# Streaming encoder step in two-pass memory attention form: splits, evictions, a row buffer, writes and norms moved to other engines and places

## The chip, the cores and the metric

One NeuronCore of a Trainium2 chip runs the whole program. The metric is the device time of one execution in microseconds (us). The core has five engines that run in parallel, each through a list of its own in fixed order: TensorE (PE, with a separate weight-load row PEld), VectorE (DVE), ScalarE (ACT), GpSimd (POOL) and SyncE (SP), which only issues transfers. 16 DMA engines move data between SBUF and HBM.

## What is computed

One layer of a streaming encoder for 2048 prompt frames and 8 x 16 sample frames of width 1024, all in float32. Cut to its core:

```
x = x + rmsnorm(y_mix, g_mix_post)           # y_mix: band attention + conv module, one output projection
h = rmsnorm(x, g_mem_pre)
x = x + rmsnorm(memory_attention(h, mk, mv, w_mq, w_mo), g_mem_post)
h = rmsnorm(x, g_ffn_pre)
f = (silu(h @ w_gate) * (h @ w_up)) @ w_down
x = x + rmsnorm(f, g_ffn_post)

def memory_attention(h, mk, mv, w_mq, w_mo):     # 4 heads of 256, 256 memory tokens
    q = h @ w_mq                                 # by heads
    s = einsum("bthd,bmhd->bhtm", q, mk) * 256 ** -0.5
    p = softmax(s)
    return (einsum("bhtm,bmhd->bthd", p, mv)) @ w_mo
```

mk and mv are rmsnorm(mem) @ w_mk and @ w_mv of the memory tokens. They and the updated caches are outputs too.

## The kernel before

**Numbers in two parts.** Every float32 operand of a matmul is split into hi (rounded to the format fp32r, by ScalarE) and lo (the rest, by VectorE or POOL, hi subtracted from the value). `mm3` issues three matmuls for each pair of operands: hi by hi, hi by lo, lo by hi (L268, L269, L270). A "form" below is such a pair of tiles.

**Seven products.** Large products are 2 x 2 blocks done with seven block products instead of eight. Each needs sums and differences of quarters of both operands; those of the weight side are b-forms, w-forms in the FFN, and those of the rows are a-forms, t-forms in the FFN.

**Who orders what.** The code is written engine by engine with tiles and pools; a scheduler then fixes the order of each engine's list. Tiles that share a place in SBUF (a `Region` gives each tag its places, in KiB, used in turn) wait for each other. An engine and SyncE's queue never overtake in their own lists: what waits holds up all behind it.

**Stages.** They follow one another, with the next one's first loads and forms let in early.

- `phase_mem` (0 to about 110 us). w_mk times the memory rows. Then w_mq is folded into mk, per head h of 4: `wload` (L256) loads two rows of w_mqT, ScalarE casts hi (L261), `lo_engine` subtracts lo (L263); 8 PSUM tiles of 6 matmuls each are evicted into `fo` times the gain (L436, VectorE). `keep(h, fo, of)` writes quarters to the HBM buffer `fs[0]`, and for heads 2 and 3 forms four sums of quarters (L401, POOL), each written too. Then w_mv and the fold of w_mo into mv, to `fs[1]`.
- `phase_proj`, attention (about 110 to 860).
- `mixout` with `cross_sample` woven in (about 860 to 1137): per tile i of 128 rows the output projection, the post-norm into the row tile `po` (L1058, VectorE), the residual added (L1059, POOL), and the write of x1 to HBM by POOL's queue (L1060). `po` has one place.
- `phase_cross` (about 1115 to 1500): 16 steps s of two row tiles each, some 22 us a step. Steps 0 to 7 multiply normed rows with the folded mk (scores), take the softmax and write it to `zs`; steps 8 to 15 multiply it with the folded mv and finish rows. `raw` loads half a b-form (L1215), `bform(halves_, j, engine)` makes form j in two halves: cast by ScalarE (L1223), lo by the engine passed (L1224). The seven b-forms of pass one are made ahead of step 0, out of loads `f1`, five ahead; those of pass two during step 7 in `between(j)`, out of loads `f2`. `aforms` makes the seven a-forms of the next step (casts L1265; lo L1266, on VectorE or POOL). `softmax` and `rows_out` are generators, stepped after every product. In `softmax` VectorE takes the maximum (L1307), ScalarE the exponentials with their sums (L1310), VectorE the reciprocals (L1313) and four scalings by head (L1315), and SyncE writes the rows (L1316). `rows_out` forms y, adds the residual (L1332) and writes the row of x2 (L1333, SyncE); in the last two steps (`done is None`) it ends there, else the normed row goes on to `forms_out`, which writes its FFN quarters to `hn`.
- For the rows that `forms_out` doesn't take, `natural(g, p)` reads x2 back (L1372), norms it (L1375 to L1379) and forms and writes quarters (POOL: L1380, L1382, L1384, L1386 with the issues between). (2, 2) is called in one piece in step 3; (2, 0) and (2, 1) are left in `self.todo`.
- `gate_up` (about 1490 to 2440): row groups g of 3, each over 22 blocks f of the hidden width. `tform` loads pieces of `hn` into the tag `nat` (L1519, three places), transposes and splits them (L1522, L1524, L1525). `wforms(f)` loads w_gate and w_up (L1531, L1532), POOL forms four sums (L1539 to L1542), ScalarE and VectorE split (L1544, L1545). In g = 0 an entry of `self.todo` is made whole behind f = 1 and f = 3. The turn to the next g re-makes the t-forms.
- `down` (about 2440 to the end).

Some of these lines shift in the changed file: L1333 there is L1332, L1519 is L1522, L1531 and L1532 are L1534 and L1535.

Of the kernel before, what the change touches and what calls it, by code (L numbers as in the profile page):

```python
# [17 lines left out]
P = 128  # L18
# [6 lines left out]
MH = 4  # L25
NM = 256
# [110 lines left out]
class Build:  # L137
# [214 lines left out]
    def phase_mem(self):  # L352
        nc, A = self.nc, self.A
# [15 lines left out]
        gk = self.t(pool, [P, KC], F32, "gk")  # L369
# [18 lines left out]
        def keep(h, fo, of):  # L388

            c, sub = h % 2, nc.gpsimd.tensor_tensor  # L390
            part = lambda j: self.fs[0][:, j, :, c * 256:(c + 1) * 256]
            temp = lambda tag: self.t(pool, [P, 4, 256], F32, tag)[:, :, :]
            if h < 2:
                nc.sync.dma_start(part(0), fo[:, :4, :])
                nc.sync.dma_start(part(2), fo[:, 4:, :])
                return
            (b11, b21), (b12, b22) = [(x[:, :4, :], x[:, 4:, :]) for x in (of[c], fo)]
            nc.sync.dma_start(part(6), b22)
            t1, t3, t2, t4 = temp("t1"), temp("t3"), temp("t1"), temp("t3")
            for j, t, x, y in ((4, t1, b12, b11), (3, t3, b22, b12), (1, t2, b22, t1), (5, t4, t2, b21)):  # L400
                sub(t, x, y, ALU.subtract)  # L401
                nc.sync.dma_start(part(j), t)

        for which, wn, on in ((0, "w_mk", "new_mem_k_promptT"), (1, "w_mv", "new_mem_v_promptT")):
            yh = self.t(pool, [P, KC, NM], F32R, "yh", 2)
            yl = self.t(pool, [P, KC, NM], F32R, "yl", 2)
            scale = 1.0 / 16.0 if which == 0 else 1.0
            for j in range(KC):
# [5 lines left out]
                ps = self.t(ps_mm, [P, 512], F32, "mm")  # L414
# [9 lines left out]
            if which == 0:  # L424
                of = []
                for h in range(MH):
                    ws = [self.wload(A["w_mqT"][2 * h + c]) for c in range(2)]
                    fo = self.t(pool, [P, KC, NM], F32, "fo")
                    of.append(fo)
                    for ic in range(KC):  # L430
                        ps = self.t(ps_mm, [P, 512], F32, "mm")
                        cc = slice(ic * P, (ic + 1) * P)
                        for c in range(2):
                            self.mm3(ps[:, :NM], ws[c][0][:, cc], ws[c][1][:, cc],
                                     yh[:, 2 * h + c, :], yl[:, 2 * h + c, :], c == 0, c == 1)
                        nc.vector.tensor_scalar(fo[:, ic, :], ps[:, :NM], gk[:, ic:ic + 1], None, ALU.mult)  # L436
                    keep(h, fo, of)
# [542 lines left out]
    def mixout(self, ctx):  # L980
# [4 lines left out]
                .at("ct", 2, (ff, [2, 10])).lay(ff, 0, ("an", 2, 1)).lay(ff, 5, ("po", 4, 1)).at("spo", 4, (ff, [22]))  # L985
# [204 lines left out]
    def phase_cross(self, ctx):  # L1190
# [27 lines left out]
        def bform(halves_, j, engine):  # L1218
            hi = self.t(pool, [P, 4, 512], F32R, f"b{j}h")
            lo = self.t(pool, [P, 4, 512], F32R, f"b{j}l")  # L1220
            for x in range(2):
                wf, c = next(halves_), slice(2 * x, 2 * x + 2)
                nc.scalar.copy(hi[:, c, :], wf[:, :, :])  # L1223
                engine.tensor_tensor(lo[:, c, :], wf[:, :, :], hi[:, c, :].bitcast(F32), ALU.subtract)  # L1224
            return hi, lo
# [74 lines left out]
        def softmax(z, t, parts):  # L1300
# [13 lines left out]
            for h in range(MH):  # L1314
                nc.vector.tensor_scalar(z[:, h, :], z[:, h, :], ri[:, h:h + 1], None, ALU.mult)  # L1315
            nc.sync.dma_start(self.zs[t], z[:, :, :].rearrange("p h n -> p (h n)"))  # L1316

        def rows_out(y, x, t, parts, done):
# [14 lines left out]
            nc.sync.dma_start(self.x2[t], x[:, :])  # L1333
# [30 lines left out]
        def natural(g, p):  # L1364
# [5 lines left out]
            for x, (t, r0) in zip((xa, xb), PAIRS[g][p][:2]):  # L1370
# [7 lines left out]
                nc.gpsimd.tensor_tensor(r[:n, :], r[:n, :], self.mhalf[:n, 0:1], ALU.pow)  # L1378
                nc.vector.scalar_tensor_tensor(x2, x2, r[:n, :], gffn[:n, :], ALU.mult, ALU.mult)  # L1379
            nc.gpsimd.tensor_tensor(tt[:, 0, :], xb[:, 0, :], xa[:, 0, :], ALU.subtract)  # L1380
            nc.gpsimd.dma_start(dst[:n, p, 0:2, :], xa)
            nc.gpsimd.tensor_tensor(tt[:, 1, :], xb[:, 1, :], tt[:, 0, :], ALU.subtract)  # L1382
            nc.gpsimd.dma_start(dst[:n, p, 4:6, :], tt)
            nc.gpsimd.tensor_tensor(xb[:, 0, :], xb[:, 1, :], xb[:, 0, :], ALU.subtract)  # L1384
            nc.gpsimd.dma_start(dst[:n, p, 2:4, :], xb)
            nc.gpsimd.tensor_tensor(xa[:, 1, :], tt[:, 1, :], xa[:, 1, :], ALU.subtract)  # L1386
            nc.gpsimd.dma_start(dst[:n, p, 6, :], xa[:, 1, :])

        self.natural = natural
# [3 lines left out]
        bf = [bform(f1, 0, nc.vector)]  # L1393
# [4 lines left out]
        bf.append(bform(f1, 1, nc.vector))  # L1398
        src[1] = fetch(1)
        for j in range(2, 7):  # L1400
            next(gen, None)
            bf.append(bform(f1, j, nc.gpsimd if j % 2 == 0 else nc.vector))
# [4 lines left out]
        for s in range(2 * n):  # L1407
# [15 lines left out]
            def between(j):  # L1423
                if j >= 0 and s == n - 1:
                    nbf.append(bform(f2, j, nc.gpsimd if j % 2 else nc.vector))
# [3 lines left out]
                if j == 4 and s == 3:  # L1429
                    self.natural(2, 2)  # L1430
# [54 lines left out]
        self.todo = [(2, 0), (2, 1)]  # L1485
# [9 lines left out]
    def gate_up(self, ctx):  # L1495
# [5 lines left out]
        pool = (Region().at("wf", 4, (sbF, [24, 28, 34.5, 38.5])).at("s", 2, (sbF, [14, 20, 22])).at("nat", 2, (sbF, [8, 10, 12]))  # L1501
# [57 lines left out]
        for g in range(3):  # L1559
            n = sum(p[2] for p in PAIRS[g])  # L1560
            for fp in range(NF // 2):
# [4 lines left out]
                for x in range(2):  # L1566
# [47 lines left out]
                    if g == 0 and x == 1 and self.todo:  # L1614
                        self.natural(*self.todo.pop(0))
# [240 lines left out]
```

## Time and profile before

| | |
|---|---|
| runs of before (median, lowest, highest of 3) | 2919.37, 2910.35, 2920.2 us |
| profiled execution, its own time | 2914.59 us |
| its span, from the first to the last instruction | 2912.8 us |
| mean granted TensorE clock | 0.993 |
| busy share of PE, DVE, ACT, POOL | 97%, 75%, 47%, 52% |
| DMA moved | 533 MB, mean 183 GB/s |

The profile is one execution, recorded by the hardware profiler. A row of instructions names the engine, the line of the kernel, out<-in, the tile's shape and a count; a bracket at the end is the idle time of the engine just before it and what released it. Memories are named by their region: sbf, sbr and sbx are parts of SBUF, flexb the parts that stages share out anew, psb is PSUM. "issue" in the chain is time in which the engine waited for nothing that the profile shows.

### The profile page before, as it was taken

The numbers are of one execution on the slowest core, as the hardware profiler recorded it, in microseconds if no ns is written. First come the engines' busy times: TensorE is split into PE (matmuls) and PEld (weight loads), VectorE is DVE, ScalarE is ACT, GpSimd is POOL, SyncE is SP. The second block draws the span as 40 slices with busy tenths as digits, with TensorE's granted clock in tenths as the row PEclk, the third lists the DMA queues.
The fourth block names the chain that finished last, engine by engine and source line by source line (L and its number), as shares of the span: only waits on it lengthen the run. The fifth ranks groups of instructions, "written<-read, shape, count | busy, mean of one in ns | idle before, by whom it ended". The sixth has DMA issues, their size and how long they took to land.

```text
span 2912.8 us, 44818 instructions
## 1 busy us (share of the span) xinstructions
PE 2835.8 (97%) x16056; PEld 2559.9 (88%) x16056; DVE 2172.3 (75%) x3232; ACT 1383.4 (47%) x2779; POOL 1506.3 (52%) x1339
## 2 busy tenths in 40 slices
PE   9999999999999998999989999999999999999998
PEld 8899999988887676788779999999999999888786
DVE  7796785889884355778778778788889997555656
ACT  4535364678883245665443333433344444332433
POOL 3458396741123447537656656455556774324413
PEclk9999999999999999999999999999999999999999
DMA  8826253576635766546664333644344446657664
GB/s 280 295 76 201 94 170 119 187 239 217 226 100 183 264 220 207 176 167 242 224 229 169 131 115 126 201 151 157 124 165 137 144 144 226 226 174 224 221 218 148
DMA packets 214818, 533.02 MB, mean 183 GB/s; under 512 B 20633, under 2 KB 95257, under 8 KB 206266
## 3 DMA queue, kind: packets, MB, share of 16 engines
q1 hardware_dynamic: 206082, 482.57, 49.9%
q0 software_dynamic: 8512, 47.58, 4.5%
q8 instruction: 126, 2.06, 0.3%
q14 instruction: 98, 0.80, 0.1%
HBM read 383.28 MB, written 154.89 MB: 185 GB/s over the span
## 4 chain that ended last, share of the span: by engine, by line
PE 75%; DVE 7%; DMA 7%; issue 4%; POOL 4%; ACT 2%; SPq 0%; DVEq 0%; POOLq 0%; ACTq 0%
PE psb L270 21%; PE psb L268 21%; PE psb L269 21%; PE psb L276 5%; PE psb L869 2%; PE psb L838 2%; PE psb L856 1%; DMA sbf<-in_w_down_dram 1%; POOL sbf L1667 1%; DMA sbf<-x 1%; DVE psb L526 1%; DVE sbr L1545 1%; DMA sbf<-hn 1%; PE psb L1522 1%; PE psb L1118 1%
## 5 line engine op out<-in xcount | busy, mean ns | idle before, releaser
L268 PE MATMUL psb<-sbr 128*128 128x384 f32 (+3 forms) x2812 | 959.3, 344 | 12.8 <-DVE flexb L436 3.8
L269 PE MATMUL psb<-sbr 128*128 128x384 f32 (+3 forms) x2644 | 898.7, 340 | 0.2
L270 PE MATMUL psb<-sbr 128*128 128x512 f32 (+2 forms) x1852 | 655.6, 355 | 3.1 <-DVE sbr L1737 2.9
L268 PEld LDWEIGHTS psb<-sbr 128*128 128x128 f32 x2812 | 530.0, 189 | 50.9 <-ACT sbr L1736 5.2
L269 PEld LDWEIGHTS psb<-sbr 128*128 128x128 f32 x2644 | 499.5, 189 | 27.0 <-DVE sbr L318 0.4
L270 PE MATMUL psb<-sbr,sbx 128*128 128x384 f32 (+3 forms) x1400 | 459.0, 329 | 2.6 <-POOL sbx L263 1.6
L1544 ACT CAST sbr<-sbf 128x512 fp32r<-128x512 f32 x360 | 222.3, 620 | 397.2 <-PE psb L269 332.5
L1545 DVE TENSOR_TENSOR sbr<-sbf,sbr 128x512 fp32r<-128x512 f32 x360 | 354.9, 988 | 52.5 <-ACT sbr L1544 51.7
L270 PEld LDWEIGHTS psb<-sbr 128*128 128x128 f32 x1852 | 347.8, 188 | 39.3 <-DVE sbr L1737 7.1
L270 PEld LDWEIGHTS psb<-sbr,sbx 128*128 128x128 f32 x1400 | 266.0, 190 | 9.9 <-POOL sbx L263 1.8
L526 DVE SCALAR_TENSOR_TENSOR psb<-sbf,psb 128x768 f32<-128x768 f32 (+1 forms) x290 | 264.2, 911 | 6.2
L1737 DVE TENSOR_TENSOR sbr<-sbf,sbr 128x384 fp32r<-128x384 f32 (+2 forms) x242 | 166.6, 712 | 84.4 <-ACT sbr L1736 83.4
L263 POOL TENSOR_TENSOR sbx<-sbf,sbr 128x1024 fp32r<-128x1024 f32 (+1 forms) x62 | 151.6, 2447 | 98.6 <-ACT sbr L261 87.4
L1667 POOL TENSOR_TENSOR sbf<-sbf 128x512 f32<-128x512 f32 x77 | 104.7, 1366 | 167.9 <-DMA sbf<-in_w_down_dram 159.4
L1736 ACT CAST sbr<-sbf 128x384 fp32r<-128x384 f32 (+2 forms) x242 | 111.6, 482 | 156.7 <-PE psb L269 129.0
L536 POOL TENSOR_TENSOR flexb<-flexb,flexb 128x128 f32<-128x128 f32 (+1 forms) x180 | 171.2, 951 | 20.6 <-ACT flexb L535 11.1
L268 PE MATMUL psb<-sbr,sbx 128*128 128x384 f32 (+2 forms) x440 | 155.6, 354 | 8.8 <-ACT sbx L1265 6.6
L261 ACT CAST sbr<-sbf 128x1024 fp32r<-128x1024 f32 x98 | 102.1, 1049 | 119.9 <-PE psb L269 83.6
L1539 POOL TENSOR_TENSOR sbf<-sbf 128x512 f32<-128x512 f32 x66 | 94.4, 1430 | 113.8 <-DVE sbr L1545 71.6
L269 PE MATMUL psb<-sbr,sbx 128*128 128x384 f32 (+2 forms) x416 | 145.3, 349 | 0.0
L535 ACT ACTIVATE flexb<-sbf 128x128 f32<-128x128 f32 (+1 forms) x180 | 104.0, 585 | 69.7 <-POOL flexb L536 64.1
L269 PE MATMUL psb<-sbx,sbr 128*128 128x512 f32 (+2 forms) x376 | 134.6, 359 | 2.3 <-DVE sbx L1525 2.0
(353 smaller groups left out, 6191.3 us busy)
## 6 DMA issues: line engine op xcount, KB each, us to landing
af<-flexb SPq DMA_DIRECT2D x33, 1344.0 KB, 5.5
sbf<-in_w_down_dram SPq DMA_DIRECT2D x154, 256.0 KB, 3.8
sbf<-in_w_up_dram SPq DMA_DIRECT2D x66, 512.0 KB, 3.7
sbf<-in_w_gate_dram SPq DMA_DIRECT2D x66, 512.0 KB, 3.8
sbf<-af SPq DMA_DIRECT2D x85, 384.0 KB, 4.3
sbf<-x SPq DMA_DIRECT2D x53, 512.0 KB, 4.2
sbf<-in_w_in_dram SPq DMA_DIRECT2D x48, 512.0 KB, 4.5
sbr<-ks POOLq DMA_DIRECT2D x16, 1024.0 KB, 8.7
```

What stands on the lines that cost most here:

```text
L263: self.lo_engine.tensor_tensor(lo[:, c], wf[:, c], hi[:, c].bitcast(F32), ALU.subtract)
L268: nc.tensor.matmul(ps, lh, rh, start=start, stop=False, **kw)
L269: nc.tensor.matmul(ps, lh, rl, start=False, stop=False, **kw)
L270: nc.tensor.matmul(ps, ll, rh, start=False, stop=stop, **kw)
L276: nc.tensor.matmul(y[o], l, r[:, o * 512:(o + 1) * 512], start=start and x == 0, stop=stop and x == 2)
L526: nc.vector.scalar_tensor_tensor(acc if w < CW - 1 else o, src(w), cwt[:, j, w:w + 1], acc, ALU.mult, ALU.add)
L536: nc.gpsimd.tensor_tensor(o, o, v, ALU.add)
L1544: nc.scalar.copy(hs[j][:, :], src[j])
L1545: nc.vector.tensor_tensor(ls[j][:, :], src[j], hs[j][:, :].bitcast(F32), ALU.subtract)
L1667: nc.gpsimd.tensor_tensor(acc[:, :], acc[:, :], q[:, :], ALU.add if s > 0 else ALU.subtract)
L1736: nc.scalar.copy(ch[:, m], a[:, x, m])
L1737: nc.vector.tensor_tensor(cl[:, m], a[:, x, m], ch[:, m].bitcast(F32), ALU.subtract)
```

## The change

1. `keep`: the four sums of heads 2 and 3 (L401) move from POOL to VectorE. The fold's evictions (L436) move from VectorE's `tensor_scalar` to ScalarE's `activation` with a scale.
2. `mixout`: `po` gets a second place. Odd tiles i go to place 0 of sbF, i = 13 to 24, i = 15 to 28; these are also places of f1.
3. `bform`: all lo splits (L1224) go to VectorE. Before, forms 2, 4 and 6 of pass one and 1, 3 and 5 of pass two went to POOL.
4. `softmax`: the four scalings by head become one `tensor_tensor` of 128 x 1024 with the reciprocals broadcast along each head.
5. `rows_out`: in the last two steps the write of x2 is issued by POOL's queue. `nat` has seven places instead of three.
6. `natural` becomes a generator with a yield after each piece. (2, 2) is put among the tails in step 2 and stepped after each product; (2, 0) and (2, 1) are chained and stepped once per f of g = 0 from f = 3 on, at most 14 steps; the turn runs what is left.

```
-            c, sub = h % 2, nc.gpsimd.tensor_tensor
+            c, sub = h % 2, nc.vector.tensor_tensor
...
-                        nc.vector.tensor_scalar(fo[:, ic, :], ps[:, :NM], gk[:, ic:ic + 1], None, ALU.mult)
+                        nc.scalar.activation(fo[:, ic, :], ps[:, :NM], AF.Copy, scale=gk[:, ic:ic + 1])
...
-                .at("ct", 2, (ff, [2, 10])).lay(ff, 0, ("an", 2, 1)).lay(ff, 5, ("po", 4, 1)).at("spo", 4, (ff, [22]))
+                .at("ct", 2, (ff, [2, 10])).lay(ff, 0, ("an", 2, 1)).at("po", 4, *[(ff, [5]), (sbF, [0])] * 6, (ff, [5]), (sbF, [24]), (ff, [5]), (sbF, [28]), (ff, [5])).at("spo", 4, (ff, [22]))
...
-        def bform(halves_, j, engine):
+        def bform(halves_, j):
...
-                engine.tensor_tensor(lo[:, c, :], wf[:, :, :], hi[:, c, :].bitcast(F32), ALU.subtract)
+                tt(lo[:, c, :], wf[:, :, :], hi[:, c, :].bitcast(F32), ALU.subtract)
...
-            for h in range(MH):
-                nc.vector.tensor_scalar(z[:, h, :], z[:, h, :], ri[:, h:h + 1], None, ALU.mult)
+            tt(z[:, :, :], z[:, :, :], ri[:, :].unsqueeze(2).to_broadcast([P, MH, NM]), ALU.mult)
...
-            nc.sync.dma_start(self.x2[t], x[:, :])
+            (nc.sync if done is not None else nc.gpsimd).dma_start(self.x2[t], x[:, :])
...
+                yield
                 nc.vector.scalar_tensor_tensor(x2, x2, r[:n, :], gffn[:n, :], ALU.mult, ALU.mult)
+                yield
             nc.gpsimd.tensor_tensor(tt[:, 0, :], xb[:, 0, :], xa[:, 0, :], ALU.subtract)
             nc.gpsimd.dma_start(dst[:n, p, 0:2, :], xa)
+            yield
...
-                if j == 4 and s == 3:
-                    self.natural(2, 2)
+                if j == 1 and s == 2:
+                    tails.append(natural(2, 2))
...
-        self.todo = [(2, 0), (2, 1)]
+        self.todo = chain(natural(2, 0), natural(2, 1))
...
-.at("nat", 2, (sbF, [8, 10, 12]))
+.at("nat", 2, (sbF, [8, 10, 12, 46.5, 48.5, 42.5, 44.5]))
...
-                    if g == 0 and x == 1 and self.todo:
-                        self.natural(*self.todo.pop(0))
+                    if g == 0 and f > 2:
+                        next(self.todo, None)
+                    if turn:
+                        for _ in self.todo:
+                            pass
```

VectorE's list in the fold of heads 0 to 2, before (L263 are the lo splits of weight rows, L421 a split of the folded operand, L436 the evictions):

```order
L263 TENSOR_TENSOR sbx<-sbf,sbr 128x1024
L436 TENSOR_SCALAR flexb_173<-psb,flexb_169 128x256
L421 SCALAR_TENSOR_TENSOR sbr<-sbf,sbr 128x256
L436 TENSOR_SCALAR flexb_173<-psb,flexb_169 128x256 x7
L263 TENSOR_TENSOR sbx<-sbf,sbr 128x1024
L436 TENSOR_SCALAR flexb_173<-psb,flexb_169 128x256
```

and ScalarE's list at the same place, after:

```order
L420 ACTIVATE sbr<-sbf 128x256
L436 ACTIVATE flexb_173<-psb,flexb_169 128x256 x7
L261 CAST sbr<-sbf 128x1024
L261 CAST sbr<-sbf 128x1024
L436 ACTIVATE flexb_173<-psb,flexb_169 128x256 x8
L261 CAST sbr<-sbf 128x1024
```

The evictions now stand between ScalarE's casts of the weight rows; VectorE's list has the L263 and the four L401 of each of heads 2 and 3 there.

VectorE's list where mixout ends and cross begins, before (L1058 is the post-norm into po, L1224 the lo splits of b-forms, L1266 those of a-forms, L1272, L1277 and L1282 sums for a-forms):

```order
L1272 TENSOR_TENSOR flexb_9882<-psb,flexb_9882 128x512
L1058 SCALAR_TENSOR_TENSOR flexb_169<-psb,flexb_169,sbf 128x512 x2
L1224 TENSOR_TENSOR sbr<-sbf,sbr 128x1024 x4
L1266 TENSOR_TENSOR sbx<-psb,sbx 128x512
L1277 TENSOR_TENSOR flexb_9882<-flexb_9882,psb 128x512
L1282 TENSOR_TENSOR flexb_9882<-psb,flexb_9882 128x512
L1266 TENSOR_TENSOR sbx<-psb,sbx 128x512
L1224 TENSOR_TENSOR sbx<-sbf,sbr 128x1024
```

and after:

```order
L1272 TENSOR_TENSOR flexb_9882<-psb,flexb_9882 128x512
L1058 SCALAR_TENSOR_TENSOR sbf<-psb,flexb_169,sbf 128x512 x2
L1224 TENSOR_TENSOR sbr<-sbf,sbr 128x1024 x7
L1266 TENSOR_TENSOR sbx<-psb,sbx 128x512
L1277 TENSOR_TENSOR flexb_9882<-flexb_9882,psb 128x512
L1282 TENSOR_TENSOR flexb_9882<-psb,flexb_9882 128x512
L1058 SCALAR_TENSOR_TENSOR flexb_169<-psb,flexb_169,sbf 128x512 x2
L1224 TENSOR_TENSOR sbx<-sbf,sbr 128x1024
```

The post-norm of this tile writes to sbf instead of the one place in flexb_169, and seven splits instead of four stand between it and the first L1266.

SyncE's queue where cross ends and gate_up begins, before (x_12 to x_15 are the last rows of x2, L1519 the loads of hn pieces for the first t-forms):

```order
L1333 DMA x_14_84_156<-sbf 128x1024
L1532 DMA sbf<-in_w_up_dram 128x1024
L1333 DMA x_12_82_154<-sbf 128x1024
L1531 DMA sbf<-in_w_gate_dram 128x1024
L1519 DMA sbf<-hn_87_159 128x512 x3
L1531 DMA sbf<-in_w_gate_dram 128x1024
L1519 DMA sbf<-hn_87_159 128x512 x2
L1532 DMA sbf<-in_w_up_dram 128x1024
L1519 DMA sbf<-hn_87_159 128x512
L1333 DMA x_15_85_157<-sbf 128x1024
```

and after (L1522, L1534 and L1535 are the same loads):

```order
L1535 DMA sbf<-in_w_up_dram 128x1024
L1522 DMA sbf<-hn_87_159 128x512 x4
L1534 DMA sbf<-in_w_gate_dram 128x1024
L1522 DMA sbf<-hn_87_159 128x512 x5
L1534 DMA sbf<-in_w_gate_dram 128x1024
L1522 DMA sbf<-hn_87_159 128x512 x2
L1535 DMA sbf<-in_w_up_dram 128x1024
```

The four writes of x2 are gone from this queue (they stand in POOL's list), and the loads of hn and of the weights follow each other.

More of the change, by code (lines that the diff above doesn't have):

```diff
@@ L1 @@
 from contextlib import ExitStack
-from itertools import islice
+from itertools import chain, islice
 import concourse.bass as bass
@@ L1397, in phase_cross @@
         next(gen)
-        bf.append(bform(f1, 1, nc.vector))
+        bf.append(bform(f1, 1))
         src[1] = fetch(1)
```

11 lines of the change are left out of this document (6 added, 5 removed).

## The prediction

> **What bounds the kernel now.** I read the page's first part, then the list of what TensorE waits for, then the windows around those waits, then the chain through the same places.
>
> ```profile
> span 2912.8 us, 44818 instructions
> PE 2835.8 (97%) x16056; PEld 2559.9 (88%) x16056; DVE 2172.3 (75%) x3232; ACT 1383.4 (47%) x2779; POOL 1506.3 (52%) x1339
> ```
>
> TensorE is busy 97% of the span, and the diff leaves its matmuls alone. So only the 2912.8 - 2835.8 = 77 us in which it stands still, and the time in which its clock is down, can be won. The waits say on whom it waited:
>
> ```profile
> PE psb L268 <- ACT sbx L1265: 6.6, 2, 5.2
> PE psb L268 <- DVE flexb L1595: 5.5, 3, 3.8
> PE psb L1522 <- DMA sbf<-hn: 5.3, 7, 1.3
> PE psb L268 <- DVE flexb L436: 3.8, 2, 2.3
> PE psb L268 <- DVE sbf L1469: 2.2, 1, 2.2
> ```
>
> The windows put them into places (columns: start:end, length, busy us and count per engine, granted clock, DMA share, GB/s):
>
> ```profile
> 50.00:60.00 10.00, 9.06 (x74) 8.66 (x72) 9.33 (x13) 3.16 (x4) 5.78 (x3) 1.00 0.99 349
> 60.00:70.00 10.00, 7.15 (x45) 6.95 (x46) 8.64 (x11) 2.26 (x3) 9.92 (x4) 0.83 0.89 271
> 70.00:110.00 40.00, 38.61 (x257) 33.86 (x256) 36.92 (x48) 22.43 (x35) 13.76 (x13) 1.00 0.94 308
> 1110.00:1120.00 10.00, 5.72 (x30) 4.62 (x28) 9.13 (x6) 4.76 (x7) 7.64 (x3) 0.92 0.40 133
> 1120.00:1130.00 10.00, 6.96 (x17) 4.77 (x18) 5.42 (x6) 3.23 (x7) 9.46 (x7) 0.57 0.87 294
> 1130.00:1140.00 10.00, 8.28 (x31) 5.90 (x31) 4.86 (x7) 8.13 (x13) 9.09 (x10) 0.83 0.70 239
> 1210.00:1260.00 50.00, 44.10 (x207) 35.47 (x206) 35.27 (x52) 28.06 (x69) 24.84 (x22) 1.00 0.54 192
> 1310.00:1330.00 20.00, 17.91 (x84) 14.38 (x83) 19.24 (x29) 13.13 (x29) 15.04 (x9) 1.00 0.86 307
> 1470.00:1510.00 40.00, 31.17 (x168) 26.55 (x166) 32.08 (x43) 20.81 (x40) 17.67 (x16) 0.96 0.69 239
> 1560.00:1570.00 10.00, 6.20 (x27) 5.88 (x27) 9.86 (x13) 2.13 (x4) 7.66 (x7) 0.83 0.54 168
> 1600.00:1650.00 50.00, 50.00 (x290) 50.00 (x289) 39.29 (x56) 18.89 (x34) 31.90 (x23) 1.00 0.36 127
> ```
>
> Idle TensorE is length minus the first busy number: 0.9 + 2.9 + 1.4 in the fold, 4.3 + 3.0 + 1.7 = 9.0 where cross begins, 5.9 and 2.1 inside it, 8.8 where gate_up begins, 3.8 soon after. That is 35 of the 77 us; the rest lies in stages the diff does not touch. Behind two of these stalls the clock is down as well. Busy time times (1 - clock) is what that costs: 0.5 + 3.0 + 1.4 = 4.9 us in 1110-1140, and 6.20 x 0.17 = 1.1 us in 1560-1570.
>
> **The change, part by part.** All gains are against the profiled execution: 2914.6 us, 1.7 us around its span.
>
> *The fold.* Eight quarter sums leave POOL for VectorE, 32 evictions leave VectorE for ScalarE.
>
> ```profile
> L401 POOL TENSOR_TENSOR flexb<-flexb x4: 2405/3362/3407, 56.6 to 71.3; 128x1024 f32<-128x1024 f32 x4
> L436 DVE TENSOR_SCALAR flexb<-psb,flexb x32: 468/474/486, 38.4 to 66.8; 128x256 f32<-128x256 f32 x32
> L263 DVE TENSOR_TENSOR sbx<-sbf,sbr x17: 1210/1215/3427, 50.6 to 110.0; 128x1024 fp32r<-128x1024 f32 x17
> L420 ACT ACTIVATE sbr<-sbf x16: 401/415/419, 18.0 to 99.9; 128x256 fp32r<-128x256 f32 x16
> 60.47 2.90 DVE sbx L263
> ```
>
> VectorE loses 32 x 0.474 = 15.2 us and gains 8 x 1.215 = 9.7 (the weight split L263 has the sum's shape). It also loses the stretch: while POOL runs L401, single L263s take up to 3.43 instead of 1.22, and the chain runs through one of them (2.90 us of it at 60.47) to the eviction at which TensorE's second stall ends; the two stalls are 3.8 us. ScalarE gains 32 evictions. Their cost there isn't in the trace; between L420's 0.41 (ScalarE, from SBUF) and the 0.47 of L436 itself (VectorE, from PSUM) I take 0.42, the row of the same engine, which is 13.4 us. In 50-70 ScalarE is busy 5.4 of 20 us, so it fits, but evictions now stand in ScalarE's line ahead of the weight casts of the next heads: 8 x 0.42 = 3.4 us of every head's 48 matmuls x 9.06/74 = 5.9 us, before its two casts of a whole weight row. That is tight. The DMA share of 0.89 to 0.99 may take the rest: whatever is won can be handed to a load. I take **3**, from 0 to 5 (its whole idle).
>
> *Two buffers for po, and the splits of the first b-forms.* The write of x1 from the one po holds VectorE up:
>
> ```profile
> 1091.16 7.49 DMA x<-flexb
>   DMA x<-flexb: 17.1, 3
> 1110.87 1.41 DVE L1058 SCALAR_TENSOR_TENSOR flexb<-psb,flexb,sbf 128x512 f32<-128x512 f32 x2 [5.82 <-DMA x<-flexb]
> 1112.20 10.03 DVE L1224 TENSOR_TENSOR sbr<-sbf,sbr 128x1024 fp32r<-128x1024 f32 x4
> 1113.44 3.72 DMA sbf<-f1s
> L1224 POOL TENSOR_TENSOR sbr<-sbf,sbr x8: 2355/2496/3383, 1117.8 to 1307.4; 128x1024 fp32r<-128x1024 f32 x8
> 1120.93 0.79 PE L268 MATMUL psb<-sbr,sbx 128*128 128x512 f32 x1 [5.21 <-ACT sbx L1265]
> ```
>
> Read downwards this is one story. L1058 waits 5.82 us for the write; the splits L1224 stand behind it; each split frees a place for the next f1 load (3.72 us); the casts of those loads stand ahead of the a-form cast L1265 on ScalarE; TensorE starts cross at 1120.93 after 5.21 us, with its clock down. With two places that wait goes, and all 14 lo splits of the head are VectorE's at 1.22 where POOL took 2.4 to 3.4. What is late next: the places at 24 and 28 of sbF, which the last po rows now use, are f1's too, so two f1 loads wait for those writes, of which one took 7.49 us before; and seven L1224 in a row now precede the L1266 that TensorE needs: 7 x 1.22 = 8.5 us if their loads are there. The start can come at most 5.2 us earlier, since mixout's last matmuls end there; the wait that goes is 5.8, the new load waits take some back: 4 of 5.2. Of the other 9.0 - 5.2 = 3.8 us of idle behind it, half: 2. Of the 4.9 of the clock, which falls with the idle ahead of it: 3. I take **9**, from 3 (2 of the 5.2 and 1 of the clock) to 13 (9.0 + 4.9, all but one).
>
> *The b-forms' splits before pass two.* Six more of them on VectorE are 6 x 1.22 = 7.3 us, most of them just ahead of and in 1310-1330, where VectorE is busy 19.24 of 20. What can cover them is the stretch that leaves with POOL's share; one group of L1315 shows it:
>
> ```profile
> 1291.77 4.94 POOL L1224 TENSOR_TENSOR sbr<-sbf,sbr 128x1024 fp32r<-128x1024 f32 x2 [8.61 <-ACT sbr L1223]
> 1294.10 5.35 DVE L1315 TENSOR_SCALAR sbf<-sbf 128x256 f32<-128x256 f32 x4
> ```
>
> It began while POOL ran two splits, and took 5.35 where four undisturbed ones take 4 x 0.336 = 1.3: 4 us back from one group. I take **-1**, from -6 (nothing relieved and all six in 1310-1330: 7.3 over 0.8 free) to +1.
>
> *Softmax.* Four scalings become one broadcast product.
>
> ```profile
> L1315 DVE TENSOR_SCALAR sbf<-sbf x64: 336/346/2552, 1157.2 to 1323.9; 128x256 f32<-128x256 f32 x64
> 1221.05 7.24 DVE L1315 TENSOR_SCALAR sbf<-sbf 128x256 f32<-128x256 f32 x4
> ```
>
> Alone that is 4 x 0.336 = 1.34 against 1.22 for a two-operand piece of 128x1024 (L263): no gain to speak of. Beside POOL four instructions can each be held, and were: 7.24 us at 1221, ahead of the 2.2 us that TensorE waited on L1469. One instruction is held once, 3.43 by the longest L263, so 3.8 us earlier at 1221. Of the 5.9 idle in 1210-1260 I take **3**, from 0 to 5. The Trainium skill, "SBUF — State Buffer", section "Who interferes with whom", says that VectorE and GpSimd share a port pair as an exclusive lock, and that an instruction with two SBUF inputs contends with it; by that page the new instruction is no safer than each of the old, only fewer, and the gain would shrink to nothing where POOL's pieces are long.
>
> *The last x2 writes.* SyncE's queue is in order; the write of a late row waits for its sum, and everything behind it waits too:
>
> ```profile
> 1464.37 4.05 DMA x<-sbf
> 1468.44 4.49 DMA sbf<-in_w_up_dram
> L1333 SPq DMA_DIRECT2D x<-sbf x16: 319/320/342, 1333.0 to 1492.7; - x16
> ```
>
> After, the four writes are POOL's and seven places for hn pieces instead of three let the loads run ahead. But the first w_up and w_gate loads land in the places those rows held, so they still wait for 4.05 us of write; POOL's own line, with a-form splits L1266 ahead, may make it later. Of 8.8 idle I take **4**, from 0 (only the waits for hn turn into waits for w_up) to 9. The Trainium skill, "DMA: Bandwidth & Descriptors", section "Issuing engines are not separate DMA queues", says that issuing from several engines saves only the sequencer's time to start the transfers; by that page this part is worth little. The trace has 4.05 us of SyncE held by a wait, which is order and not a start.
>
> *Late norms stepwise.* Before, a whole norm goes into POOL's line at once:
>
> ```profile
> 1543.63 1.66 POOL L1380 TENSOR_TENSOR sbf<-sbf 128x512 f32<-128x512 f32 x1 [0.84 <-DVE sbf L1379]
> L1387 POOL DMA_DIRECT2D hn<-sbf x3: 536/544/573, 1201.6 to 1560.9; - x3
> 1565.00 0.44 PE L268 MATMUL psb<-flexb,sbr 128*128 128x384 f32 x1 [3.81 <-DVE flexb L1595]
> ```
>
> Its four subtractions and four issues (up to 1.7 and 0.6 each, 9 us) stand between the weights' quarter sums, the last issue at 1560.9, and TensorE stands 3.81 us at 1565. A step per f adds at most 2.3 us to POOL. An f is 7 products of 4 x 3 matmuls, 84, at 290 in 50 us 14.5; POOL is busy 31.90 of 50 in 1600-1650, so 5.2 us are free in each. I take **4** of 3.8 + 1.1, from 0 to 5.
>
> **Sum:** 3 + 9 - 1 + 3 + 4 + 4 = 22, so 2914.6 - 22 = 2892.6. The profiled execution is 4.8 us under the median of 2919.4 (2910.4 to 2920.2); half of that put back gives **2895**. The ends: all low terms give -3, all high ones 38; as they fail independently, half of the way to each end is the forecast's own case: 10 to 30 us, 2887 to 2907.
>
> **Rivals.**
>
> *The idle only moves* (0.17). The f1 load at 28 lands late and TensorE waits 4 of its 5.21 us there; loads set the fold's pace; w_up is as late as before. Terms 1 + 3 - 3 + 1 + 1 + 4 = 7: 2914.6 - 7 + 2.4 = 2910. For it: DMA shares of 0.87 to 0.99 in those windows. Against: at 1110-1120 the share is 0.40.
>
> *It does not do what it says* (0.07). POOL keeps L1266 and the x scaling, so VectorE's stretches stay; fold and softmax give 0, pass two's splits -5, the rest 9 + 4 + 0: 8, or 2909. Against: POOL's eight L1224 alone take 2.4 to 3.4 us each, and those leave.
>
> *Moving the writes gives nothing* (0.08). The first w_up and w_gate loads wait for the same four writes, whoever issues them, and the hn loads that run ahead only queue in front of w_up. What is saved is four issues of 0.32 us on SyncE, 1.3, so the term falls from 4 to 1: 2898. This is the rule of the DMA page named above.
>
> *Slower: the steps cost each f* (0.08). One POOL step (1.7 + 0.6) falls ahead of the quarter sums in each of 14 f, and the forms reach TensorE late. If the lead of the sums is under 2.3 us in every f, it costs 14 x 2.3 = 32, and with the clock's 1.05 of 1560-1570 each time 15 more. 47 - 18 from the other parts: 2914.6 + 29 = 2944. For it: VectorE 39 of 50 and POOL 32 of 50 busy in g = 0. Against: TensorE is busy 50.00 of 50 there, and a whole norm in one piece cost only 4.9 once.
>
> **How the numbers follow.** The forecast has 0.60. A measurement of this kernel tells about 0.5%, 14.6 us, from no change, so faster means under 2904.8: the forecast without the 0.04 of it that lies above, and the DMA rule, 0.64. Within: those 0.04, idle moved and VectorE still held, 0.28. Slower: 0.08. The range leaves out the slower case and a little at each end: 2882 (a gain of 35, near the sum of the high ends) to 2915.
>
> **What would show it.** Fold: no L436 in TensorE's waits, no L263 over 1.3 in 55-75. Cross: no wait of L1058 for a write, its first product after under 2 us of idle, clock 1.00 in the two windows behind. Softmax: the product under 3.5 everywhere. gate_up: fewer waits for hn, the first w_up load earlier. Norms: 1560-1570 full. Wrong: TensorE's idle in cross or gate_up as large as now under another name, or a new wait in each f of g = 0.

## The result, and the profile after

| | before | changed |
|---|---|---|
| median of 6 runs, us | 2915.61 (2910.35 to 2920.2) | 2897.86 (2892.33 to 2904.06) |
| ratio to before | 1 | 0.9939, interval 0.9921 to 0.9956 |
| profiled execution, us | 2914.59 | 2894.95 |
| its span, us | 2912.8 | 2893.2 |
| mean clock | 0.993 | 0.996 |

The medians are of six runs each; the table ahead of the prediction had three of before. The change makes the kernel faster by 0.6%, 17.8 us between the medians. The forecast was 2895, the range 2882 to 2915. The profile's first lines after:

```profile
span 2893.2 us, 44781 instructions
PE 2824.9 (98%) x16056; PEld 2553.6 (88%) x16056; DVE 2164.3 (75%) x3172; ACT 1397.7 (48%) x2811; POOL 1475.8 (51%) x1323
```

TensorE stands still 68.3 us instead of 77, and its busy time, for the same 16056 matmuls, is 10.9 us less, most of it by the clock (0.996 instead of 0.993). What it waits for now, by line (us in total, times, longest):

```profile
PE psb L268 <- DVE flexb L1598: 5.3, 3, 3.3
PE psb L268 <- DVE sbf L1462: 3.7, 1, 3.7
PE psb L1525 <- DVE sbr L1528: 3.5, 1, 3.5
PE psb L268 <- ACT flexb L436: 1.7, 2, 1.6
```

Of the waits shown before, those on L1265 (6.6) and on hn (5.3) are gone from the top. L1598 is L1595 of before, and it is as long as it was: the stall after the late norms has not left. L1462 is new, and so is the wait of L1525 for L1528, a split of a t-form, just before 1460. The same windows, moved to where the work now lies:

```profile
50.00:60.00 10.00, 8.27 (x67) 7.87 (x66) 6.29 (x6) 7.75 (x16) 0.00 (x0) 1.00 1.01 347
60.00:70.00 10.00, 10.00 (x86) 10.00 (x85) 9.96 (x10) 5.23 (x9) 0.00 (x0) 1.00 1.05 345
70.00:110.00 40.00, 36.17 (x233) 31.14 (x232) 35.32 (x53) 24.84 (x40) 6.65 (x12) 1.00 0.90 307
1110.00:1120.00 10.00, 7.70 (x32) 5.88 (x31) 10.00 (x11) 7.24 (x13) 4.30 (x6) 0.85 0.80 289
1120.00:1130.00 10.00, 10.00 (x49) 8.26 (x48) 7.74 (x7) 4.90 (x8) 9.83 (x6) 0.98 0.77 252
1350.00:1360.00 10.00, 6.28 (x28) 5.02 (x27) 7.20 (x8) 5.51 (x11) 9.66 (x9) 0.83 0.59 216
1500.00:1510.00 10.00, 7.88 (x43) 6.91 (x41) 9.74 (x9) 4.07 (x8) 8.94 (x9) 1.00 0.42 152
1510.00:1520.00 10.00, 4.88 (x17) 4.37 (x18) 9.97 (x12) 0.62 (x1) 5.99 (x6) 0.65 0.38 135
```

The start of cross is repaired: 2.3 us of idle in 1110-1130 where 7.3 were, 81 matmuls instead of 47. In the fold the idle moved from 60-70 to 70-110 (3.8 us there, 1.4 before). And 1500-1520 has lost 7.2 us, with a clock of 0.65.

To see where the time came from, I read from both traces when certain matmuls start: the first of attention (L838), the first of mixout (L1003), the first of a step of cross (84 matmuls of L268 to L270 with 512 columns make a step) and of a block f (84 with 384 columns). Times between such marks, in us; the last three columns are profiles of experiments below:

| stretch | before | changed | difference | one_po | pool_splits | forced_steps |
|---|---|---|---|---|---|---|
| start to attention | 615.1 | 615.2 | +0.1 | 615.2 | 613.0 | 612.7 |
| attention to mixout | 256.5 | 256.9 | +0.4 | 255.7 | 256.3 | 255.9 |
| mixout to step 1 of cross | 280.2 | 268.9 | -11.3 | 278.3 | 276.3 | 271.6 |
| step 1 to 7 | 133.0 | 128.9 | -4.1 | 129.6 | 126.5 | 130.8 |
| step 7 to 14 | 148.6 | 153.2 | +4.6 | 152.7 | 148.6 | 153.9 |
| step 14 to f = 6 of gate_up | 161.2 | 153.6 | -7.6 | 156.9 | 159.1 | 144.0 |
| f = 6 to the end | 1318.2 | 1316.5 | -1.7 | 1317.0 | 1318.1 | 1319.3 |

Ten profiles share the new fold with all its loads, and in them attention starts at 612.4 to 617.3: a spread of 4.9 us where the kernels do the same. In most later stretches the profiles that an edit does not touch spread by 3 to 5 us as well (mixout to step 1: 268.7 to 272.9 in the eleven kernels with both of its changes; step 7 to 14 is steadier). So a smaller difference between two profiles shows nothing by itself.

### The profile page after: what moved, and what is told of

The parts are those of the page before. It is cut to its first block, busy times and chain, and to the rows that moved or that the text cites. A ratio compares the mean times of both kernels' runs of the same rounds, so it can differ in the third digit from the quotient of the medians.

```text
span 2893.2 us, 44781 instructions
## 1 busy us (share of the span) xinstructions
PE 2824.9 (98%) x16056; PEld 2553.6 (88%) x16056; DVE 2164.3 (75%) x3172; ACT 1397.7 (48%) x2811; POOL 1475.8 (51%) x1323
## 4 chain that ended last, share of the span: by engine, by line
PE 74%; DVE 8%; DMA 6%; POOL 5%; issue 4%; ACT 3%; SPq 0%; DVEq 0%; POOLq 0%; ACTq 0%
PE psb L268 20%; PE psb L270 20%; PE psb L269 20%; PE psb L276 7%; PE psb L869 2%; PE psb L838 2%; PE psb L856 2%; DMA sbf<-in_w_down_dram 1%; POOL sbf L1673 1%; DMA sbf<-x 1%; DVE sbr L1548 1%; DVE psb L526 1%; PE psb L1118 1%; PE psb L1525 1%; DVE sbr L1743 1%
## 5 line engine op out<-in xcount | busy, mean ns | idle before, releaser
L268 PE MATMUL psb<-sbr 128*128 128x384 f32 (+3 forms) x2812 | 959.3, 344 | 13.0 <-ACT sbr L1742 3.0
L270 PE MATMUL psb<-sbr 128*128 128x512 f32 (+2 forms) x1852 | 654.9, 355 | 2.1 <-DVE sbr L1743 1.9
L268 PEld LDWEIGHTS psb<-sbr 128*128 128x128 f32 x2812 | 528.6, 188 | 51.4 <-ACT sbr L1742 5.0
L270 PE MATMUL psb<-sbr,sbx 128*128 128x384 f32 (+3 forms) x1400 | 457.8, 328 | 3.4 <-POOL sbx L263 2.1
L1548 DVE TENSOR_TENSOR sbr<-sbf,sbr 128x512 fp32r<-128x512 f32 x360 | 365.7, 1019 | 51.6 <-ACT sbr L1547 49.4
L270 PEld LDWEIGHTS psb<-sbr 128*128 128x128 f32 x1852 | 347.2, 188 | 38.2 <-DVE sbr L1743 6.1
L270 PEld LDWEIGHTS psb<-sbr,sbx 128*128 128x128 f32 x1400 | 264.6, 189 | 10.1 <-POOL sbx L263 2.6
L263 POOL TENSOR_TENSOR sbx<-sbf,sbr 128x1024 fp32r<-128x1024 f32 (+1 forms) x62 | 151.3, 2443 | 107.3 <-ACT sbr L261 99.1
L1673 POOL TENSOR_TENSOR sbf<-sbf 128x512 f32<-128x512 f32 x77 | 106.8, 1394 | 165.8 <-DMA sbf<-in_w_down_dram 164.1
L1742 ACT CAST sbr<-sbf 128x384 fp32r<-128x384 f32 (+2 forms) x242 | 112.3, 482 | 160.3 <-PE psb L269 133.2
L268 PE MATMUL psb<-sbr,sbx 128*128 128x384 f32 (+2 forms) x440 | 154.2, 351 | 1.9 <-DVE sbf L1325 1.0
L1542 POOL TENSOR_TENSOR sbf<-sbf 128x512 f32<-128x512 f32 x66 | 98.2, 1487 | 111.9 <-DVE sbr L1548 71.0
```

What stands on the lines that cost most here:

```text
L263: self.lo_engine.tensor_tensor(lo[:, c], wf[:, c], hi[:, c].bitcast(F32), ALU.subtract)
L268: nc.tensor.matmul(ps, lh, rh, start=start, stop=False, **kw)
L270: nc.tensor.matmul(ps, ll, rh, start=False, stop=stop, **kw)
L1548: nc.vector.tensor_tensor(ls[j][:, :], src[j], hs[j][:, :].bitcast(F32), ALU.subtract)
L1673: nc.gpsimd.tensor_tensor(acc[:, :], acc[:, :], q[:, :], ALU.add if s > 0 else ALU.subtract)
L1742: nc.scalar.copy(ch[:, m], a[:, x, m])
```

## The experiments

All are the changed kernel with one edit; forced_whole22 and fewer_old_fold join two. Ratios are to the kernel before, on the same chip. The first four ran on one chip (before 2919.4), the next four on another (2920.5), the last four on a third (2919.7). The changed kernel was run beside them on the third chip only (changed_again); elsewhere it is compared by its ratio, 0.9939 both times.

**one_po**: `po` back in one place.

```
-.at("po", 4, *[(ff, [5]), (sbF, [0])] * 6, (ff, [5]), (sbF, [24]), (ff, [5]), (sbF, [28]), (ff, [5]))
+.lay(ff, 5, ("po", 4, 1))
```

> The changed kernel with po back in one place; all else as changed. If the second place is what won the head of cross, TensorE's idle at the start of cross comes back: VectorE waits for the write of x1 again (three waits of 4 to 7 us), TensorE starts cross after some 5 us of idle at a lowered clock, and the eleven us that the second step starts earlier shrink to 3 or less: about 2906. Rival: the splits moved from POOL to VectorE won it; then this kernel keeps at least 8 of the 11 us: about 2899.

2906.9 us, ratio 0.9957 (0.9941 to 0.9974): about 5 us slower than the changed kernel by the ratios, whose intervals overlap. The trace is clearer. VectorE's waits for the write and TensorE's two stalls are back, in the timeline of this run:

```profile
1111.36 1.41 DVE L1058 SCALAR_TENSOR_TENSOR flexb<-psb,flexb,sbf 128x512 f32<-128x512 f32 x2 [6.32 <-DMA x<-flexb]
1121.27 0.79 PE L268 MATMUL psb<-sbr,sbx 128*128 128x512 f32 x1 [5.52 <-ACT sbx L1265]
1125.75 0.79 PE L270 MATMUL psb<-sbr,sbx 128*128 128x512 f32 x1 [3.26 <-DVE sbx L1266]
```

In the changed kernel the same matmuls waited far less:

```profile
1115.05 0.50 PE L268 MATMUL psb<-sbr,sbx 128*128 128x512 f32 x1 [0.92 <-ACT sbx L1265]
1117.16 0.80 PE L270 MATMUL psb<-sbr,sbx 128*128 128x512 f32 x1 [1.39 <-DVE sbx L1266]
```

Mixout to step 1 takes 278.3, 9.4 more than changed and 5.4 above the highest of the eleven. The second place is needed.

**pool_splits**: the lo splits of b-forms back on POOL.

```
...
-                bf.append(bform(f1, j))
+                bf.append(bform(f1, j, nc.gpsimd if j % 2 == 0 else nc.vector))
...
-                    nbf.append(bform(f2, j))
+                    nbf.append(bform(f2, j, nc.gpsimd if j % 2 else nc.vector))
```

> The changed kernel with the lo splits of b-forms back on POOL where they were (forms 2, 4, 6 of pass one; 1, 3, 5 of pass two). If po's wait was the whole cause, the start of cross moves by under 2 us and only pass one's last step gets about 1 us back: 2897. Rival: the splits share the gain; POOL's splits of 2.4 to 3.4 us make the a-form and b-form chain late, and the second step starts 4 us or more later than in the changed kernel: 2902 or more.

2899.2 us, ratio 0.9932 (0.9917 to 0.9947): by the time, no loss. By the trace both theories were half right:

```profile
1115.66 7.03 POOL L1224 TENSOR_TENSOR sbr<-sbf,sbr 128x1024 fp32r<-128x1024 f32 x3
1115.89 0.50 PE L268 MATMUL psb<-sbr,sbx 128*128 128x512 f32 x1 [0.92 <-ACT sbx L1265]
1122.96 0.50 PE L268 MATMUL psb<-sbr,sbx 128*128 128x512 f32 x1 [3.34 <-ACT sbx L1265]
```

Cross starts on time, but its second product waits 3.34 us beside three POOL splits in a row, and mixout to step 1 takes 276.3, 7.4 more than changed and 3.4 above the highest of the eleven. The 9.4 and 7.4 add up to more than the 11.3 that both changes won together: with either of them undone, most of the chain stands again. The loss is given back later: step 7 to 14 takes 148.6, as before the change, and the wait on L1462 is absent; the start of gate_up then takes 5.5 more.

**four_scalings**: four scalings a tile again.

```
-            tt(z[:, :, :], z[:, :, :], ri[:, :].unsqueeze(2).to_broadcast([P, MH, NM]), ALU.mult)
+            for h in range(MH):
+                nc.vector.tensor_scalar(z[:, h, :], z[:, h, :], ri[:, h:h + 1], None, ALU.mult)
```

> The changed kernel with the four scalings per row tile in place of the broadcast product. If the product is what won 4 us between steps 1 and 7, groups of four beside POOL reach 5 us or more again and TensorE's waits of 2 us in pass one come back: 2901 to 2902. Rival: these waits left because the work before them moved, and the four scalings cost nothing on the path: 2898.

2902.5 us, ratio 0.9942 (0.9928 to 0.9957), which the time alone does not tell from 0.9939. The groups on VectorE, first of this run, then of the changed kernel (busy us, mean ns; L1315 and L1314 are the same place of the code):

```profile
L1315 DVE TENSOR_SCALAR sbf<-sbf 128x256 f32<-128x256 f32 x64 | 41.6, 712 | 0.4
```

```profile
L1314 DVE TENSOR_TENSOR sbf<-sbf 128x1024 f32<-128x1024 f32 x16 | 23.0, 1436 | 0.4
```

The broadcast product saves 18.6 us of VectorE. One group of four scalings, at 1187, again took 8.30 us, TensorE again waited 3.3 us on the eviction behind it (at 1196), and step 1 to 7 takes 132.4, 3.5 more than changed. The twelve profiles with the product spread from 126.5 to 130.8 there, so 1.6 of this lie above the highest of them. Here too the wait on L1462 is absent afterwards, and the start of gate_up is longer (158.4).

**forced_steps**: each piece of the late norms is queued on POOL behind the quarter sum issued just before it in the code.

```
-            tt(src[6], g[:, 1, :], src[1], ALU.subtract)
+            self.last_sum = tt(src[6], g[:, 1, :], src[1], ALU.subtract)
...
-                        next(self.todo, None)
+                        with self.tc.issue_after(self.last_sum.ins):
+                            next(self.todo, None)
```

> The changed kernel in which each piece of the late norms is queued on POOL behind the last quarter sum of the weights' forms made just before, so that the pieces really stand one per f. In the changed kernel's list the first of the two norms stands in one block ahead of the quarter sums. If that block makes the three stalls of 1.6, 2.1 and 3.4 us at 1503 to 1518 and the low clock behind them, they go, and 6 to 9 us are won: 2889 to 2892. Rival: these stalls come from weights that land late, and stay: 2898.

2890.1 us, ratio 0.9899 (0.9884 to 0.9914). What it takes away is seen in the changed kernel's POOL, where the pieces of norm (2, 0) follow each other, the four subtractions (L1381 to L1390) ahead of the quarter sum L1542:

```profile
1502.93 1.59 POOL L1381 TENSOR_TENSOR sbf<-sbf 128x512 f32<-128x512 f32 x1 [0.88 <-issue]
1504.60 1.62 POOL L1384 TENSOR_TENSOR sbf<-sbf 128x512 f32<-128x512 f32 x1
1506.17 1.60 POOL L1387 TENSOR_TENSOR sbf<-sbf 128x512 f32<-128x512 f32 x1
1507.72 0.57 POOL L1385 DMA_DIRECT2D hn<-sbf  x1
1508.32 1.30 POOL L1390 TENSOR_TENSOR sbf<-sbf 128x512 f32<-128x512 f32 x1
1509.57 1.26 POOL L1542 TENSOR_TENSOR sbf<-sbf 128x512 f32<-128x512 f32 x1
1511.78 0.45 PE L268 MATMUL psb<-sbr 128*128 128x384 f32 x1 [2.05 <-DVE flexb L1592]
1517.78 0.69 PE L268 MATMUL psb<-flexb,sbr 128*128 128x384 f32 x1 [3.35 <-DVE flexb L1598]
```

With the steps forced, the same stretch is full:

```profile
1500.00:1510.00 10.00, 9.24 (x53) 8.92 (x52) 10.00 (x15) 5.79 (x12) 5.15 (x4) 1.00 0.25 91
1510.00:1520.00 10.00, 10.00 (x59) 10.00 (x59) 9.32 (x15) 4.41 (x8) 5.46 (x5) 1.00 0.31 105
```

112 matmuls in 20 us instead of 60. Step 14 to f = 6 takes 144.0 instead of 153.6.

**old_fold**: the fold as before.

```
-            c, sub = h % 2, nc.vector.tensor_tensor
+            c, sub = h % 2, nc.gpsimd.tensor_tensor
...
-                        nc.scalar.activation(fo[:, ic, :], ps[:, :NM], AF.Copy, scale=gk[:, ic:ic + 1])
+                        nc.vector.tensor_scalar(fo[:, ic, :], ps[:, :NM], gk[:, ic:ic + 1], None, ALU.mult)
```

> The changed kernel with the fold as before: quarter sums on POOL, evictions on VectorE. By the two traces attention starts at the same time in both (615.1 and 615.2 us), so the fold's part would be worth nothing and this kernel takes 2898. Rival, the prediction's term: 3 us, so 2901, with attention starting 3 us later.

2897.3 us, ratio 0.9920 (0.9905 to 0.9934); attention starts at 615.7. That is within the spread of the new fold, and the time is no longer: the fold's part shows no gain here.

**whole_norms**: `natural` in one piece, (2, 2) in step 3, the others behind f = 1 and f = 3.

```
-                if j == 1 and s == 2:
-                    tails.append(natural(2, 2))
+                if j == 4 and s == 3:
+                    for _ in natural(2, 2):
+                        pass
...
-                    if g == 0 and f > 2:
-                        next(self.todo, None)
-                    if turn:
-                        for _ in self.todo:
+                    if g == 0 and x == 1 and self.todo:
+                        for _ in self.todo.pop(0):
+                            pass
```

> The changed kernel with the late norms made whole as before: (2, 2) in step 3, (2, 0) and (2, 1) behind f = 1 and f = 3. If the steps only moved one block from the wrong place to another, 2898 and TensorE stands some 4 us near f = 4. Rival, the prediction's term: 4 us, 2902.

2896.2 us, ratio 0.9914 (0.9900 to 0.9929): no slower than the changed kernel's 0.9939. TensorE's stalls lie at the same place:

```profile
1502.01 0.49 PE L268 MATMUL psb<-sbr 128*128 128x384 f32 x1 [1.64 <-DVE flexb L1588]
1515.87 0.67 PE L268 MATMUL psb<-flexb,sbr 128*128 128x384 f32 x1 [3.97 <-DVE flexb L1599]
```

So the yields, as the scheduler used them, changed nothing for the first norm.

**sync_writes**: the last x2 writes back in SyncE's queue.

```
-            (nc.sync if done is not None else nc.gpsimd).dma_start(self.x2[t], x[:, :])
+            nc.sync.dma_start(self.x2[t], x[:, :])
```

> The changed kernel with the last four writes of x2 back in SyncE's queue; nat keeps seven places. If the writes held the queue up, the first blocks of gate_up start 4 us or more later (f = 1 at 1494 or later instead of 1490.3): up to 2902. Rival, the rule that another issuing queue saves only the start: within 1 us, 2898.

2897.6 us, ratio 0.9917 (0.9900 to 0.9934): no loss in the time. f = 1 does start late, at 1498.4 instead of 1490.3. But 3.7 of these 8.1 us were lost ahead of step 14, where the edit changes nothing; step 14 to f = 1 takes 71.6 instead of 67.2. A write stands in the chain again, here ahead of the load L1371 that reads rows back for a late norm:

```profile
1490.18 6.51 DMA x<-sbf
```

The next blocks then take less (f = 1 to f = 6: 83.7 instead of 86.4); step 14 to f = 6 is 155.3, 1.7 more than changed, which is within the spread. The Trainium skill, "DMA: Bandwidth & Descriptors", section "Issuing engines are not separate DMA queues", says that issuing from several engines at once saves only the time that it takes to start the transfers. For the whole time this run agrees with it. For the 4.4 us between step 14 and f = 1, in one profile, it does not.

**three_nat**: three places for hn pieces.

```
-.at("nat", 2, (sbF, [8, 10, 12, 46.5, 48.5, 42.5, 44.5]))
+.at("nat", 2, (sbF, [8, 10, 12]))
```

> The changed kernel with three places for hn pieces; the writes stay on POOL. If the depth of these loads is what won the start of gate_up and the turns, TensorE's waits for hn come back (5 us in all before), f = 1 starts 4 us later and the turns lose 2: 2902 or more. Rival: the queue's order alone won it: 2898.

2908.5 us, ratio 0.9956 (0.9941 to 0.9971), 11 to 12 us above the other three of this chip. The waits for hn are back:

```profile
PE psb L268 <- DMA sbf<-hn: 5.4, 1, 5.4
PE psb L1525 <- DMA sbf<-hn: 1.8, 1, 1.8
```

Step 14 to f = 6 takes 160.3, 6.7 more than changed and nearly before's 161.2. The rest of the 10.5 us between the two profiles, 4.0, lies ahead of step 14, where the edit changes nothing. The seven places are the larger part of what won the start of gate_up, and the only one that the time shows.

**changed_again**: the changed kernel, unedited.

> The changed kernel itself, beside the other three on one chip, so that its own spread and its ratio to before are known there. Both theories: 0.992 to 0.994 of before, the start of attention within 2 us of before's 615.1, since the loads of the first stage land differently from run to run.

2900.3 us, ratio 0.9939 (0.9927 to 0.9951), attention at 616.4.

**forced_whole22**: the edit of forced_steps, and (2, 2) whole in step 3.

```
-                if j == 1 and s == 2:
-                    tails.append(natural(2, 2))
+                if j == 4 and s == 3:
+                    for _ in natural(2, 2):
+                        pass
```

> The forced steps for (2, 0) and (2, 1), and (2, 2) made whole in step 3 as before. If the gain of the forced steps is the order on POOL at the start of gate_up and nothing else, it is 8 to 10 us under the changed kernel run beside it, and f = 3 to f = 6 lie as in the forced steps. Rival: the tail (2, 2) was worth something too, 2 to 3 us; then only 6 us remain.

2886.8 us, ratio 0.9892 (0.9879 to 0.9905): 13.5 us under the changed kernel on the same chip, intervals apart, and the fastest of all. f = 3 starts at 1523.7 and f = 6 at 1567.4 (forced_steps 1525.3 and 1568.9). No gain of the tail (2, 2) is seen.

**fewer_loads** and **fewer_old_fold**: every second load of w_mv and w_mo is left out, and the row loaded before is cast and split in its place; with the new and with the old fold.

```
-        wf = self.t(self.w, [P, D], F32, "wf")
-        nc.sync.dma_start(wf[:, :], src)
+        if src is not None:
+            self.kept_wf = self.t(self.w, [P, D], F32, "wf")
+            nc.sync.dma_start(self.kept_wf[:, :], src)
+        wf = self.kept_wf
...
-                    ws = [self.wload(A["w_mo"][2 * h + c]) for c in range(2)]
+                    ws = [self.wload(A["w_mo"][2 * h] if c == 0 else None) for c in range(2)]
...
```

> The changed kernel without every second load of w_mv and w_mo in the first stage (the casts and splits are made of the row loaded before, so their outputs are those of the wrong rows; every other instruction stays): 8 loads of 0.5 MB less. If loads pace the first stage, so that the fold's gain was handed to them, attention starts 4 us or more earlier than in the changed kernel, and 2 to 4 us earlier than in the same kernel with the old fold. Rival: ScalarE's line (evictions ahead of casts) paces it; then the start moves by under 2 us.

> The same fewer loads (the same part left out), with the old fold: quarter sums on POOL and evictions on VectorE. If loads pace the stage with the new fold only, this one keeps its two stalls of 3.8 us behind VectorE and starts attention 2 to 4 us later than the kernel with fewer loads and the new fold. Rival: the fold is worth nothing even without the loads; both start together.

2895.3 us (0.9918, 0.9905 to 0.9931) and 2896.8 us (0.9926, 0.9914 to 0.9938): the times do not part them. The traces differ at the first matmul of attention (L840 here; start of the first and of the last), new fold first:

```profile
L840 PE MATMUL psb<-sbr x448: 221/334/689, 609.6 to 842.7; 128*128 128x256 f32 x69, 128*128 128x384 f32 x69, 128*128 128x128 f32 x6, 128*128 128x512 f32 x6
```

```profile
L840 PE MATMUL psb<-sbr x448: 221/335/735, 615.5 to 848.7; 128*128 128x256 f32 x69, 128*128 128x384 f32 x69, 128*128 128x128 f32 x6, 128*128 128x512 f32 x6
62.41 0.58 PE L270 MATMUL psb<-sbr 128*128 128x256 f32 x1 [2.32 <-DVE flexb L438]
```

With the loads out, the new fold starts attention at 609.6, 2.8 below the earliest of the ten with all loads; the old one keeps its stalls of 1.43 and 2.32 us and gains nothing. 5.9 us lie between them, in one profile each, where the spread is 4.9. TensorE's idle in 50-110 points the same way: 5.2 us before, 5.6 changed, 2.1 with fewer loads and the new fold, 4.0 with fewer loads and the old one.

## Why the prediction was right, and which steps were not

The sum was right: 22 us forecast against the profiled execution, 19.6 measured (2914.6 to 2895.0), and 17.8 between the medians. Its terms less so, and that their errors cancelled was luck.

- **Start of cross, 9: right in mechanism, measured 11.3.** The chain from the write through L1058, the splits, the f1 loads and L1265 was the cause; one_po and pool_splits each put most of it back (9.4 and 7.4). The feared new wait, f1 loads behind po's writes at 24 and 28, did not show: TensorE's first wait is 0.92 us.
- **Softmax, 3: right as far as it shows, 4.1 less and 3.5 back with four_scalings**, each in one profile, of which 2.2 and 1.6 lie above the highest of the twelve with the product. The new instruction's mean is 1.44 us, its longest 2.61. The Trainium skill, "SBUF — State Buffer", section "Who interferes with whom", says that an instruction of VectorE with two SBUF inputs contends with a GpSimd instruction that reads SBUF. The trace agrees as far as it goes: 4 of the 16 products, all beside work of POOL, took 1.66 to 2.61 us, the other 12 took 1.21 to 1.23. Of the 64 scalings before, 17 took 0.98 to 2.55 us instead of 0.34: one product is held about as often as one scaling was, and there are a quarter as many.
- **Start of gate_up, 4 for writes and places, 4 for norms: the total right (7.6), the shares wrong.** Step 14 to f = 1 takes 67.2 us instead of 79.4, 12.2 less; f = 1 to f = 6 takes 86.4 instead of 81.8, 4.6 more. Undone alone, the places for hn cost 6.7 up to f = 6; the writes cost 1.7 at most there and nothing in the time. I had argued the term from the write in SyncE's queue; for the writes the rival "moving the writes gives nothing" came true, as far as the time shows. In the changed kernel, too, a load of w_up in SyncE's queue waits 4.9 us for a write of x2.
- **Late norms: the step that failed.** "A step per f adds at most 2.3 us to POOL" took the yields for the order. The scheduler set the first norm's pieces one after the other at 1502.9 to 1511.9, with a single quarter sum among them, as in whole_norms, and the stall of 3.81 at 1565 came back as 2.05 and 3.35 at 1512 and 1518, with the clock at 0.65. So the term, put at 4, was nothing: f = 1 to f = 6 got 4.6 longer, and whole_norms takes the same there (86.7). The order of POOL's list is fixed before a kernel runs and would have told. Forced into place, the steps are worth 9.6 us between step 14 and f = 6. The slower rival, steps that cost each f, is refuted: forced_steps loses 2.0 us once between f = 8 and f = 12, and nothing in the other blocks.
- **Fold, 3: wrong, no gain that shows over the spread.** The stalls behind L263 did leave; its longest is now 1.23 us:

```profile
L263 DVE TENSOR_TENSOR sbx<-sbf,sbr x17: 1209/1217/1226, 49.7 to 109.7; 128x1024 fp32r<-128x1024 f32 x17
L436 ACT ACTIVATE flexb<-psb,flexb x32: 458/475/492, 38.2 to 64.0; 128x256 f32<-128x256 f32 x32
50.92 6.10 DMA sbf<-in_w_mv_dram
57.11 1.04 ACT sbr L261
58.16 0.38 ACT flexb L436
58.59 0.38 PE L268 MATMUL psb<-sbr 128*128 128x256 f32 x1 [1.57 <-ACT flexb L436]
```

  The chain tells what took the place of one: a load of w_mv, the cast that waits for it on ScalarE, and behind that cast an eviction for which TensorE stands 1.57 us. The 3.8 us of idle in 70-110 are several short waits, 1.6 on L263 the most; that each goes back to a load is not shown. The bound 0, "whatever is won can be handed to a load", held, and the fewer loads speak for it, in one profile each. The eviction costs 0.475 on ScalarE, not the 0.42 I took.
- **Splits of pass two, -1: step 7 to 14 lost 4.6, for another reason.** Steps 7 and 8 got no slower (41.8 us, before 44.9, with POOL's splits 41.9), so VectorE was not overloaded there. The largest loss is step 10, 26.4 instead of 21.9, with one wait of 3.72 us on L1462 at 1355 and the clock at 0.83; what the other steps gain and lose cancels. L1462 stands in VectorE's line behind a normed row, L1337, that waits for POOL's L286:

```profile
1352.06 2.28 DVE L1337 SCALAR_TENSOR_TENSOR sbf<-sbf,flexb 128x1024 f32<-128x1024 f32 x1 [1.59 <-POOL sbf L286]
1354.26 0.67 DVE L1462 TENSOR_TENSOR sbf<-sbf,psb 128x512 f32<-128x512 f32 x1
```

  It is absent with the splits on POOL and with four scalings. Why either edit moves it is open; an order of the scheduler is likely and was not tried.

Of the signs that the prediction named, two did not come: L436 still stands among TensorE's waits (1.7, now on ScalarE), and 1560-1570 is not full (9.03). One came in part: the clock where cross begins is 0.85 in 1110-1120 and 0.98 in 1120-1130.

The rival "the idle only moves" came true in the fold and at f = 2. The terms' errors, -3 and -3.6 against +2.3 and +1, and 1.7 less behind f = 6, mostly cancelled. Undoing the fold, the steps or the moved writes alone costs no time that shows; what the traces tie to a gain is the second place for po, the splits of the first b-forms, the places for hn and, more weakly, the broadcast product. Of these the time alone shows the places for hn and, less surely, the second place for po.

## What to carry to other kernels

A yield or a later line in the code is no place in an engine's list where a scheduler sets the order: read the list, and tie what must wait to the instruction it must follow. Two edits on one chain are not two terms: undo each alone before sharing out the gain. Before costing a stall as won, see what the next wait would be; in the fold, with transfers 0.9 to 1.0 busy, it was in part a load.

## What the runs showed of the hardware

An eviction of 128x256 with a scale takes 0.475 us on ScalarE and 0.474 on VectorE: no difference, so that choice is here only about whose line is free. Idle cost more than its length: in 1510-1520 of the changed kernel 5.1 us of idle left 17 matmuls of 384 columns in 10 us where 59 stand in the same window of forced_steps. At 10.00 / 59 = 0.17 us each, the 4.9 us of busy time would have held 29; the granted clock of 0.65 takes most of the rest (0.65 x 29 = 19).
